# Hybrid decoder layer on one core: attention by half chunks in two turns, TensorE in program order

## The chip, the cores and the metric

The kernel runs on one core of one Trainium2 chip. The metric is the device time of one launch in microseconds (us), taken as the median of several runs; lower is better. The core has a matrix engine (TensorE, in the profile PE for its matmuls and PEld for its weight loads), three engines for elementwise work (VectorE, in the profile DVE; ScalarE, ACT; GpSimd, POOL) and a queue engine (SyncE, SP). [...]

## The reference: what is computed

One inference step of one decoder layer, for a new sequence of 4096 tokens and for 64 sample tokens (8 sequences of 8) with caches. The core of it, cut to what matters here:

```
h = rmsnorm(x, g_pre);  z = h @ w_in                  # 1024 -> combined projection
out_a = silu(g) * B * conv3(C * h_in)                 # 256 channels
out_b = silu(ag) * window_attention(q, k, v, sink)    # 8 heads in 2 kv groups, window 128, 128-query blocks
out_c = silu(mg) * memory_attention(mq, mk, mv)       # 4 heads, 256 memory tokens
y = concat(out_a, out_b, out_c) @ w_out               # width 1024 -> 1024
x = x + rmsnorm(y, g_post)
```

Both attentions are softmax attentions with head size 64. The window softmax has one extra sink logit per head, and a query block of 128 tokens sees its own block and the one before it.

## The kernel before, in words

**Precision.** fp32 values are split into a high and a low float32r part (names ending in hi/lo, mh/ml), and a product is made of three or four matmuls of parts. The scores use full 128-row operands: 64 rows carry the high and 64 rows the low part of a query, against keys stored likewise (`load_queries`, L1115; `load_keys`, L1100).

**Stages.** `input_projection` (L936) does the combined projection in three phases (matmuls at L368) and puts queries, keys, values and gates into DRAM. In its third phase it also makes the memory keys and values and the attention of chunk 0. `open_attention` (L1004) then opens the pools of the last stage. In this stage the output projection of 33 blocks of 128 tokens (`Block.run`, L1476; 32 blocks of the prompt, one of the sample tokens) is interleaved with the attention of chunks 1 to 15 (256 tokens, two half chunks each).

**A block of the output projection.** Its input, the gated mix, is split into mh and ml (`Block.split`, L1461). Two accumulations of 128x512 (p = 0, 1) have 24 matmuls each: for k = 0 to 7 three of them (mh, ml, mh against the high, high, low part of w_out, L1492). The result is multiplied by the norm's gain on VectorE (L1499), squared and summed on ScalarE (L1500); then come a power on GpSimd (L1506), the residual sum on VectorE (L1510) and the store.

**The attention before.** It comes in units. A window unit (`window_unit`, L1237) is one block of 128 queries and one kv group: 8 score matmuls 128x256 into two one-bank tiles `ws` (L1246); a copy and a predicated copy out of PSUM per tile (L1248, L1249); the softmax on VectorE and ScalarE (L1251 to L1264: maximum, exponentials, sum, reciprocal, product); 4 transposes (L1269); a copy (L1271) and two masks on GpSimd (L1276, L1279). A memory unit (`cross_unit`, L1173) is one head of a chunk: 4 score matmuls 128x256 (L1182), maximum, exponentials (L1183 to L1187), the factors on GpSimd (L1191), 4 transposes (L1197) and two copies (L1201). The products with the values are made per half chunk (L1088 for the memory, L1218 and L1224 for the window) into one two-bank tile, followed by the gates on VectorE (L1227, L1170). The class `Pipe` (L1050) hands out one unit at each call of `start` (L1525), and in later calls its factors, transposes and products.

**What sets the order.** `Block.run` calls `start` at k = 2 and k = 6 of each accumulation, in blocks 0 and 1 at k = 0, 2, 4, 6. The order on all engines in this stage is then set by the framework's scheduler, TensorE's too, from priorities in the program's order and its own estimates; on each engine instructions run strictly in the order that results. PSUM has four pools in this stage: `s` (scores) and `t` (transposes) of two one-bank tiles each, `z` (output products) of two one-bank tiles, `pv` (values) of one two-bank tile. GpSimd issues the loads of queries and keys (L1110, L1121), SyncE the others. From block 26 on, the attention of the sample tokens is done in steps at the same calls (`late_start`, L1562).

## Time and profile before

| what | value |
|---|---|
| median of 3 runs | 1538.47 us (1533.01 to 1540.08) |
| the profiled execution's own time | 1536.4 us |
| its span, first to last instruction | 1534.7 us |
| granted TensorE clock | 1.0 of full speed |
| first output product matmul | at 931.2 us of the span |
| last output product matmul | at 1528.2 us of the span |

The profile was taken in one execution. The busy shares are those of the whole span; a busy PE is not PE at its peak, since the ends of matmuls are modelled and matmuls overlap. So where the prediction needs the cost of a matmul it takes the distance from one start to the next, and where it needs a chain on the other engines it takes durations. Rows of the views have the source line of the kernel before, the engine, the operation, output and inputs by tile name, and shapes.

### The profile page before, as it was taken

The numbers are of one execution on the slowest core, as the hardware profiler recorded it, in microseconds if no ns is written. First come the engines' busy times: TensorE is split into PE (matmuls) and PEld (weight loads), VectorE is DVE, ScalarE is ACT, GpSimd is POOL, SyncE is SP. The second block draws the span as 40 slices with busy tenths as digits, with TensorE's granted clock in tenths as the row PEclk, the third lists the DMA queues.
The fourth block names the chain that finished last, engine by engine and source line by source line (L and its number), as shares of the span: only waits on it lengthen the run. The fifth ranks groups of instructions, "written<-read, shape, count | busy, mean of one in ns | idle before, by whom it ended". The sixth has DMA issues, their size and how long they took to land.

```text
span 1534.7 us, 30168 instructions
## 1 busy us (share of the span) xinstructions
PE 1521.5 (99%) x11341; PEld 1399.5 (91%) x11341; DVE 1145.5 (75%) x2055; ACT 805.7 (52%) x2039; POOL 376.1 (25%) x603
## 2 busy tenths in 40 slices
PE   9999999999999999999999999999999999999998
PEld 9999999999999999999999998788888888888877
DVE  6788887899988777897777678766666666666743
ACT  6675665475322222354454447655666556565632
POOL 0223332211300000000101203544444444444310
PEclk9999999999999999999999999999999999999999
DMA  9989999878855333677877789977777777777333
GB/s 265 194 222 225 283 284 266 272 242 298 193 181 180 126 126 126 220 230 280 227 273 230 229 293 254 231 161 153 156 148 148 151 162 149 158 160 150 130 110 96
DMA packets 177942, 306.28 MB, mean 200 GB/s; under 512 B 33925, under 2 KB 107653, under 8 KB 177765
## 3 DMA queue, kind: packets, MB, share of 16 engines
q1 hardware_dynamic: 130901, 227.38, 48.2%
q0 software_dynamic: 46176, 75.92, 25.5%
q8 instruction: 90, 1.47, 0.4%
q10 hardware_dynamic: 720, 1.05, 0.2%
q14 instruction: 55, 0.45, 0.1%
HBM read 197.23 MB, written 108.05 MB: 199 GB/s over the span
## 4 chain that ended last, share of the span: by engine, by line
PE 86%; DMA 7%; DVE 4%; issue 1%; ACT 1%; POOL 1%; SPq 0%; ACTq 0%; DVEq 0%; POOLq 0%
PE c L368 47%; PE y L1492 23%; PE ws L1246 4%; DMA nat<-in_x_p 3%; DMA md<-th 2%; PE wo L1088 2%; PE wt L1269 2%; PE xs L1182 2%; PE xt L1197 2%; PE wo L1218 2%; PE wo L1224 1%; PE mem_acc L789 1%; DMA qd<-z 1%; DVE z L375 1%; DMA xr<-in_x_p 0%
## 5 line engine op out<-in xcount | busy, mean ns | idle before, releaser
L1492 PE MATMUL y<-wo,mh 128*128 128x512 f32 (+1 forms) x1040 | 349.8, 399 | 0.0
L375 DVE TENSOR_TENSOR z<-c,z 128x520 f32<-128x520 f32 (+1 forms) x308 | 194.5, 646 | 79.2 <-PE c L368 78.2
L1492 PEld LDWEIGHTS y<-wo,mh 128*128 128x128 f32 x1040 | 194.3, 188 | 39.2 <-issue 2.4
L1492 PE MATMUL y<-wo,ml 128*128 128x512 f32 (+1 forms) x520 | 201.6, 388 | 0.0
L1259 ACT ACTIVATE sm<-sm,wnm 128x128 f32<-128x128 f32 x256 | 99.5, 390 | 61.0 <-DVE wnm L1253 60.2
L1191 POOL TENSOR_SCALAR xp<-xp,xrd 128x256 f32<-128x256 f32 x128 | 74.4, 588 | 209.6 <-DVE xrd L1187 209.6
L1492 PEld LDWEIGHTS y<-wo,ml 128*128 128x128 f32 x520 | 98.2, 189 | 16.3
L1183 DVE TENSOR_REDUCE xmx<-xs 128x2 f32<-128x512 f32 x64 | 44.1, 689 | 59.2 <-PE xs L1182 59.1
L1271 ACT COPY wpt<-wt 128x512 f32<-128x512 f32 x64 | 37.3, 582 | 88.1 <-PE wt L1269 85.6
L1246 PEld LDWEIGHTS ws<-kst,q 128*128 128x128 f32 x512 | 69.9, 190 | 5.3 <-ACT xp L1186 0.7
L1499 DVE TENSOR_TENSOR yn<-y,gpost 128x512 f32<-128x512 f32 (+1 forms) x66 | 45.1, 683 | 39.6 <-PE y L1492 39.3
L1246 PE MATMUL ws<-kst,q 128*128 128x256 f32 x512 | 73.0, 283 | 0.4 <-ACT xp L1186 0.4
L1500 ACT ACTIVATE y<-y 128x512 f32<-128x512 f32 (+1 forms) x66 | 38.6, 584 | 64.2 <-DVE yn L1499 64.2
L737 POOL CAST wmask<-negs 128x256 uint8<-128x256 f32 x1 | 0.9, 864 | 268.3 <-ACT z L377 268.3
L1279 POOL TENSOR_SCALAR_AFFINE_SELECT wpt<-wpt 128x512 f32<-128x512 f32 x64 | 52.7, 824 | 42.1 <-ACT wpt L1271 39.1
L1186 ACT ACTIVATE xp<-xs,xnm 128x256 f32<-128x256 f32 x128 | 58.8, 464 | 7.1 <-DVE xnm L1184 7.1
L1121 POOL DMA_DIRECT2D q<-qd x64 | 42.8, 674 | 70.6 <-DVE wo L186 60.9
L276 ACT ACTIVATE nat<-nat 104x1024 f32<-104x1024 f32 x40 | 42.3, 1057 | 26.1 <-DMA nat<-in_x_p 26.1
L1510 DVE SCALAR_TENSOR_TENSOR xr<-yn,yst,xr 128x1024 f32<-128x1024 f32 (+2 forms) x34 | 43.4, 1280 | 15.5 <-POOL yst L1506 13.2
L1110 POOL DMA_DIRECT2D kst<-qd x64 | 38.6, 616 | 63.5 <-PE xt L1197 41.4
L1249 DVE COPY_PREDICATED sm<-wmask,ws 128x256 f32<-128x256 uint8 x124 | 52.2, 437 | 2.5 <-ACT sm L1248 2.1
L1276 POOL TENSOR_SCALAR_AFFINE_SELECT wpv<-wpt 128x512 f32<-128x512 f32 x62 | 40.2, 648 | 50.6 <-ACT wpt L1271 50.5
(961 smaller groups left out, 5095.5 us busy)
## 6 DMA issues: line engine op xcount, KB each, us to landing
q<-qd POOLq DMA_DIRECT2D x64, 384.0 KB, 7.9
xr<-in_x_p SPq DMA_DIRECT2D x32, 512.0 KB
nat<-in_x_p SPq DMA_DIRECT2D x39, 416.0 KB
o_yp<-xr SPq DMA_DIRECT2D x31, 512.0 KB
md<-th POOLq DMA_DIRECT2D x48, 260.0 KB, 7.9
qd<-zh SPq DMA_DIRECT2D x48, 260.0 KB
qd<-z SPq DMA_DIRECT2D x48, 260.0 KB
kst<-qd POOLq DMA_DIRECT2D x60, 192.0 KB, 5.6
```

The source lines that it names most:

```text
L368: TE.matmul(bank[:, :HW], l, r, start=first and i == 0, stop=last and i == 3 * KH - 1)
L375: add = lambda dst, other: V.tensor_tensor(dst, c, other, op=ALU.add)
L1183: V.tensor_reduce(mx[:, :nb], s, axis=AX.X, op=ALU.max)
L1186: S.activation(p[:, i, :], s[:, i, :], AF.Exp, bias=nm[:, i : i + 1], scale=SCALE, accum_out=den[:, i : i + 1])
L1191: G.tensor_scalar(p[:, i, :], p[:, i, :], rd[:, i : i + 1], 0.5, op0=ALU.mult, op1=ALU.mult)
L1246: TE.matmul(s3[:, hh, :], self.q[:, 4 + 2 * (2 * half + hh) + kvh, i * P : i * P + P], self.kst[:, 2 * kvh + part, i * P : i * P + 2 * P], ...
L1249: V.copy_predicated(sm[:, 2 * half : 2 * half + 2, :], third["wmask"], third["negs"] if first else s3[:, :, 0:P])
L1259: S.activation(sm[:, hh, :], sm[:, hh, :], AF.Exp, bias=nm[:, hh : hh + 1], scale=SCALE, accum_out=den[:, hh : hh + 1])
L1279: G.affine_select(p3, p3, pattern=[[0, 4], [1, P]], compare_op=ALU.is_ge, fill=0.0, base=0, channel_multiplier=-1)
L1492: TE.matmul(acc, self.hl[l][:, k], wo[k][c0 // 512][:, r, c0 % 512 : c0 % 512 + c1 - c0], start=j == 0, stop=j == passes * KT - 1)
L1499: V.tensor_tensor(yn[:m, c0:c1], acc[:m], gpost[:m, c0:c1], op=ALU.mult)
L1510: V.scalar_tensor_tensor(self.xr[:m, cs], yn[:m, cs], st[:m, 3:4], self.xr[:m, cs], op0=ALU.mult, op1=ALU.add)
```

## The change

The attention of the last stage is no longer handed out in units. A half chunk (128 tokens) h is done in two turns, each put between output product matmuls:

- `first_half(h)`: all 16 window score matmuls of the half chunk, into two two-bank tiles, then the 8 transposes of the memory probabilities of half chunk h-1. Then the softmax of the window scores: one copy and one predicated copy of 512 columns per kv group, where there were two of 256. It also starts the loads for the next chunk.
- `second_half(h)`: the 8 memory score matmuls of two heads into one two-bank tile and their softmax, the value products of half chunk h-1, on every second half chunk 2 transposes of the values, and the 8 transposes of the window probabilities; then masks and gates.

The turns of half chunk b + 4 stand in block b at p = 0, k = 4 and at p = 1, k = 4. For the first ones a table, `EARLY`, sets closer places: counted in k's of the output product (16 to a block), half chunk 2 has its turns at 4 and 12, 3 at 14 and 20, 4 at 22 and 28, 5 at 30 and 36, 6 at 38 and 44.

TensorE's order is as written from block 0 to block 25 (`manual_schedule` on PE); from block 26 on, and on the other engines everywhere, the scheduler orders as before. PSUM in this stage: pool `w` of two two-bank tiles (window scores, window transposes and value products in turn), pool `x` of one two-bank tile (memory scores and memory transposes in turn), pool `z` of two one-bank tiles. The queries of a chunk are loaded by six DMAs in place of four, of the same bytes in sum, in another order of halves. The steps of the sample tokens stand at k = 1 and 3 in place of 2 and 6. The number of matmuls is the same in both programs (10901), and TensorE's order is the same up to the first output product, but for 8 window score matmuls that stood ahead of it before.

```diff
-        ps = {tag: ctx.enter_context(tc.tile_pool(name=f"ps{tag}", bufs=1 if tag == "pv" else 2, space=bass.MemoryType.PSUM))
-              for tag in ("s", "t", "z", "pv")}
+        ps = {tag: ctx.enter_context(tc.tile_pool(name=f"ps{tag}", bufs=n, space=bass.MemoryType.PSUM))
+              for tag, n in (("w", 2), ("x", 1), ("z", 2))}
...
+    def two_banks(tag, name):
+        return ps[tag].tile([P, 2, 512], F32, tag=tag, name=name)
...
+            heads = lambda part, j, ts: qd[part, j : j + 2, :, ts].rearrange("j (v d) n -> d j v n", v=2)
             for part in range(2):
-                for hh in range(2):
-                    half = hh if part == 0 else 1 - hh
-                    G.dma_start(self.q[half * 64 : half * 64 + 64, hh::2, :],
-                                  qd[part, 1:7, hh * 64 : hh * 64 + 64, self.ts].rearrange("j p n -> p j n"))
+                for n, (i, j) in enumerate(((0, 1), (4, 3), (8, 5))):
+                    half = (n == 2) ^ part
+                    G.dma_start(self.q[64 * half : 64 * half + 64, i : i + 4, :].rearrange("p (j v) n -> p j v n", v=2),
+                                heads(part, j, self.ts))
...
+        def window_scores(self, i):
+            b = 2 * self.c + i
+            w = [two_banks("w", f"ws{b}_{kvh}") for kvh in range(2)]
...
+            for kvh, col, bank in sorted(tasks):
+                for part in range(2):
+                    TE.matmul(out(kvh, col, bank), q(kvh, col, bank), k(kvh, part), start=part == 0, stop=part == 1)
+            self.ws = w
+
+        def window_probabilities(self, i):
...
+                S.copy(sm4, s4[:, :, :, P : 2 * P])
+                V.copy_predicated(sm4, third["wmask"].unsqueeze(1).to_broadcast([P, 2, 2, P]), s4[:, :, :, 0:P])
+                self.window_softmax(b, kvh, sm)
...
+        def memory_scores(self, i):
+            c, nb = self.c, CT // P
+            x = two_banks("x", f"xs{c}_{i}").rearrange("p h (b k) -> p h b k", b=nb)
...
+            self.xps = [self.cross_softmax(2 * i + hh, x[:, hh]) for hh in range(2)]
+
+        def memory_transposes(self, i):
+            c, self.pts = self.c, [[], []]
+            tx = two_banks("x", f"xt{c}_{i}")
...
+                (S.copy if hh else V.tensor_copy)(pt, tx[:, hh].rearrange("p (a n) -> p a n", a=2))
+
+        def window_turns(self, i):
+            b = 2 * self.c + i
+            self.steps = [[], []]
+            tw = two_banks("w", f"wt{b}")
+            for kvh in range(2):
+                for hh in range(4):
+                    TE.transpose(tw[:, kvh, hh * P : (hh + 1) * P], self.sms[kvh][:, hh, :], ident)
+            for kvh in range(2):
+                self.window_masks(b, kvh, tw[:, kvh], self.steps[kvh])
...
                 for k in range(KT):
-                    if k in starts:
-                        start()
+                    starts.get((p, k), lambda: None)()
...
+    def first_half(h):
+
+        c, i = divmod(h, 2)
+        if c < NCH:
+            chunks[c].window_scores(i)
+        if 2 < h <= 2 * NCH:
+            chunks[(h - 1) // 2].memory_transposes((h - 1) % 2)
+        if c < NCH:
+            chunks[c].window_probabilities(i)
+            if i == 0:
+                chunks[c].values(chunks[c - 1].vts[2])
+                chunk_load(c + 1)
+            elif c + 1 < NCH:
+                chunks[c + 1].load_mix()
+
+    def second_half(h):
+
+        c, i = divmod(h, 2)
+        if c < NCH:
+            chunks[c].memory_scores(i)
+        banks = None
+        if 2 < h <= 2 * NCH:
+            banks = chunks[(h - 1) // 2].products((h - 1) % 2)
...
+        if c < NCH:
+            chunks[c].window_turns(i)
+        if 2 < h <= 2 * NCH:
+            chunks[(h - 1) // 2].gates((h - 1) % 2, banks)
...
+    EARLY = {4: (first_half, 2), 12: (second_half, 2), 14: (first_half, 3), 20: (second_half, 3), 22: (first_half, 4),
+             28: (second_half, 4), 30: (first_half, 5), 36: (second_half, 5), 38: (first_half, 6)}
+
+    def starts_of(b):
+        steps = {n - 16 * b: (f_, h) for n, (f_, h) in EARLY.items() if n // 16 == b}
+        if b >= 2:
+            steps |= {4: (first_half, b + 4), 12: (second_half, b + 4)} if b > 2 else {12: (second_half, b + 4)}
+        return {(n // 8, n % 8): lambda f_=f_, h=h: f_(h) for n, (f_, h) in steps.items()}
...
+    turn = ExitStack()
+    turn.enter_context(tc.manual_schedule(engines={mybir.EngineType.PE}))
     for i in range(31):
-        run(i, late_start if i >= 26 else start, (0, 2, 4, 6) if i < 2 else (2, 6))
+        if i == 26:
+            turn.close()
+        starts = starts_of(i)
+        run(i, starts | ({(p, k): late for p in range(2) for k in (1, 3)} if i >= 26 else {}))
```

On the other engines the order that the scheduler makes of the changed program is, in the regular blocks, for one half chunk. ScalarE: two copies of window scores, copy of a memory transpose tile, 8 window exponentials, square of y_0, 4 memory exponentials, two copies of window transposes, cast mh of the next block, square of y_1. VectorE: predicated copy, maximum, copy of the other memory transpose tile, predicated copy, maximum, y_0 times gain, the two sums, reciprocals and products of the window softmax, the memory maxima (the reciprocal of the first head's sum stands between them), the two gates, y_1 times gain, ml of the next block, residual sum. GpSimd: factors of the memory probabilities, four masks, the power, and between them ten DMA issues per chunk.

More of the change, by code (lines that the diff above doesn't have):

```diff
@@ new lines, in memory_scores @@
+        def memory_scores(self, i):
+            c, nb = self.c, CT // P
+            x = two_banks("x", f"xs{c}_{i}").rearrange("p h (b k) -> p h b k", b=nb)
+            for hh in range(2):
+                q = self.q[:, 2 * i + hh]
+                for n in range(nb):
+                    for part in range(2):
+                        TE.matmul(x[:, hh, n], q[:, n * P : n * P + P], third["mk"][:, part, 2 * i + hh, :], start=part == 0, stop=part == 1)
+            self.xps = [self.cross_softmax(2 * i + hh, x[:, hh]) for hh in range(2)]
@@ new lines, in window_turns, with products @@
+        def window_turns(self, i):
+            b = 2 * self.c + i
+            self.steps = [[], []]
+            tw = two_banks("w", f"wt{b}")
+            for kvh in range(2):
+                for hh in range(4):
+                    TE.transpose(tw[:, kvh, hh * P : (hh + 1) * P], self.sms[kvh][:, hh, :], ident)
+            for kvh in range(2):
+                self.window_masks(b, kvh, tw[:, kvh], self.steps[kvh])
+        def products(self, i):
+            c = self.c
+            banks = two_banks("w", f"wo{c}_{i}")
+            o = banks[:, 0, CT:]
+            both_values(o, *([(third["mkv"][:, kt, 256 + i * P : 256 + (i + 1) * P], self.pts[hh][kt]) for kt in range(2)]
+                             for hh in range(2)))
+            self.band_values(i, self.steps, banks[:, :, :CT], gated=False)
+            return banks
@@ L1474, in split, with run @@
             self.hl = [hi, lo]
-        def run(self, last, start, split, starts):
+        def run(self, last, starts):
             b, m = self.b, self.m
@@ L1550, in run @@
             blocks[i].split()
-        blocks[i].run(i == len(blocks) - 1, start, split if i == 1 else lambda: None, starts)
+        if i == 1:
+            starts[1, 4] = lambda before=starts[1, 4]: (before(), split())
+        blocks[i].run(i == len(blocks) - 1, starts)
     stages = [sample_mem(0), sample_mem(1), sample_window()]
@@ L1560, in hybrid_layer, with late @@
     quarter = [0]
-    def late_start():
-        start()
+    def late():
         if quarter[0] == 0:
```

162 lines of the change are left out of this document (85 added, 77 removed).

## Prediction

> **What bounds the kernel now.** I read the page first, then the busy time by stretches, then the order in time of each engine where the change is.
>
> ```profile
> PE 1521.5 (99%) x11341; PEld 1399.5 (91%) x11341; DVE 1145.5 (75%) x2055; ACT 805.7 (52%) x2039; POOL 376.1 (25%) x603
> PE 86%; DMA 7%; DVE 4%; issue 1%; ACT 1%; POOL 1%; SPq 0%; ACTq 0%; DVEq 0%; POOLq 0%
> ```
>
> The first line is the busy time of each engine, the second the chain that ended last: TensorE sets the end. The stretches (length, then busy time of PE, PEld, DVE, ACT, POOL, granted clock, DMA) tell where it does not:
>
> ```profile
> 945.00:960.00 15.00, 13.23 (x89) 9.82 (x90) 10.91 (x32) 10.54 (x44) 9.56 (x17) 1.00 1.10 319
> ...
> 1000.00:1400.00 400.00, 400.00 (x2467) 327.17 (x2465) 270.17 (x677) 238.08 (x876) 182.43 (x283) 1.00 0.77 154
> ...
> 1520.00:1535.00 15.00, 8.43 (x60) 7.77 (x58) 4.72 (x9) 1.72 (x7) 1.10 (x2) 0.95 0.29 88
> ```
>
> In the stage that changes (from 930 us) TensorE never rests from 1000 to 1400 us. It waits at the stage's start, and at its end, which the change leaves alone. But a busy TensorE may hide slack, so I read the starts of its matmuls, in a stretch with one of everything (start, duration, count):
>
> ```profile
> 1099.73 1.00 PE L1246 MATMUL ws<-kst,q 128*128 128x256 f32 x7
> 1100.57 0.60 PE L1197 MATMUL xt<-ident,xp 128*128 128x128 f32 x4
> 1100.93 0.47 PE L1492 MATMUL y<-wo,mh 128*128 128x512 f32 x1
> 1101.24 0.40 PE L1492 MATMUL y<-wo,ml 128*128 128x512 f32 x1
> 1101.48 0.62 PE L1492 MATMUL y<-wo,mh 128*128 128x512 f32 x2
> 1101.94 0.39 PE L1492 MATMUL y<-wo,ml 128*128 128x512 f32 x1
> 1102.17 0.62 PE L1492 MATMUL y<-wo,mh 128*128 128x512 f32 x2
> ...
> 1103.78 0.63 PE L1182 MATMUL xs<-mk,q 128*128 128x256 f32 x4
> 1104.34 1.08 PE L1088 MATMUL wo<-xpt,mkv 128*64 128x256 f32 x8
> ...
> 1106.81 0.66 PE L1269 MATMUL wt<-ident,sm 128*128 128x128 f32 x4
> ```
>
> A window score takes 0.12 us (0.84 for 7), an output product 0.23 (0.69 for three from 1101.48), a memory score 0.12, the values of a half chunk 2.47 (1104.34 to 1106.81) and 0.09 before them. Four transposes and the first product after them take 0.67 (1100.57 to 1101.24); less 0.23 that leaves 0.11 each. So a block with its half chunk needs 48 x 0.23 + 16 x 0.12 + 8 x 0.12 + 17 x 0.11 + 2.56 = 18.35 us. It has 113 matmul records; 2467 of them in 400 us are 18.3 us a block. Sum and measurement agree: going from product to attention and back costs nothing, and there is no hidden wait.
>
> [...]
>
> **The change part by part.** The sum is made against the profiled execution's own 1536.4 us (span 1534.7); the median of the runs is 2.1 us above that.
>
> *Fewer groups, other order.* Both builds have 10901 matmuls. By the sum above the regular blocks stay at 18.35 us, as long as nothing makes TensorE wait: 0 us.
>
> *Waits in regular blocks.* TensorE is in program order now, so a late operand stops the products behind it. These rows price the chains (out, in, count, busy us, mean ns):
>
> ```profile
> L1191 POOL TENSOR_SCALAR xp<-xp,xrd 128x256 f32<-128x256 f32 x20 | 12.3, 621 | 33.8 <-DVE xrd L1187 33.8
> L1186 ACT ACTIVATE xp<-xs,xnm 128x256 f32<-128x256 f32 x22 | 10.1, 463 | 0.0
> L1249 DVE COPY_PREDICATED sm<-wmask,ws 128x256 f32<-128x256 uint8 x22 | 9.3, 434 | 0.0
> L1264 DVE TENSOR_TENSOR sm<-sm,wrd 128x512 f32<-128x512 f32 x12 | 8.2, 687 | 0.2
> L1510 DVE SCALAR_TENSOR_TENSOR xr<-yn,yst,xr 128x1024 f32<-128x1024 f32 x6 | 7.7, 1285 | 2.2 <-POOL yst L1506 2.2
> L1183 DVE TENSOR_REDUCE xmx<-xs 128x2 f32<-128x512 f32 x11 | 7.6, 689 | 12.2 <-PE xs L1182 12.2
> L1500 ACT ACTIVATE y<-y 128x512 f32<-128x512 f32 x11 | 6.5, 588 | 11.0 <-DVE yn L1499 11.0
> L1271 ACT COPY wpt<-wt 128x512 f32<-128x512 f32 x11 | 6.4, 583 | 16.7 <-PE wt L1269 16.7
> L1201 DVE COPY xpt<-xt 128x256 f32<-128x256 f32 x11 | 4.6, 420 | 1.9 <-PE xt L1197 1.9
> L1506 POOL TENSOR_TENSOR yst<-yst,mhalf 128x1 f32<-128x1 f32 x5 | 2.8, 564 | 0.0
> L1263 DVE RECIPROCAL wrd<-wden 128x4 f32<-128x4 f32 x12 | 2.1, 178 | 0.4
> ```
> ```profile
> 1208.90 0.40 ACT L1259 ACTIVATE sm<-sm,wnm 128x128 f32<-128x128 f32 x1 [1.32 <-DVE wnm L1253]
> ...
> 1210.37 0.19 ACT L1259 ACTIVATION_READ_ACCUMULATOR sm<-sm,wnm 128x1 f32 x1
> ```
>
> Four window exponentials take 1.66 us, first start to last end. Two forms are new: a 512-column copy on ScalarE (I take 0.58 of L1271) and a 512-column predicated copy. That lies between one and two of 0.434; I take 0.70, since 256 columns more cost 0.27 (0.420 against 0.687).
>
> Time from the start of a first turn: the scores end at 0.96 and 1.92. First kv group: copy to 1.75, predicated copy 2.45, maximum (as L1183) 3.15, copy of the memory transposes that stands next on VectorE 3.85, small operation 4.0, exponentials 6.0; second group's exponentials 7.7; sum, reciprocal, product (0.18 + 0.18 + 0.69) 8.75. TensorE wants it after 1.92 + 0.88 (transposes) + 24 x 0.23 + 0.96 + 2.56 + 0.44 = 12.3: **3.5 us early**. Memory: scores end at 9.5; maximum and small operation 10.4, two exponentials 11.5, reciprocal, second maximum 12.5, exponentials 13.7, reciprocal and factors 15.1; wanted at 18.35 + 1.92 = 20.3. Copies of the window transposes end at 14.9; the tile is wanted at 19.3. The slowest tail is the output's: y_1 ends at 15.7; gain (0.69), square (0.59 + 0.19), sum, power (0.56, perhaps behind a DMA issue of 0.7), residual (1.29) end by 19.9, and the next predicated copy, behind it on VectorE, is wanted at 20.1. Lateness there does not add up from block to block, since each round starts from TensorE's y_1. So 0 us.
>
> *The start.* The dense stretch has 14 kinds of matmul rows from 930.2 to 990 us, of which these are the first and the last, and the causes of the waits:
>
> ```profile
> L1492 PE MATMUL y<-wo,mh 128*128 128x512 f32 x76 | 26.2, 402 | 0.0
> ...
> L368 PE MATMUL c<-hi_7T,w_2A 128*128 128x260 f32 x1 | 0.3, 282 | 0.0
> ```
> ```profile
> 932.44 3.75 DVE L409 TENSOR_TENSOR z<-z,zh 128x520 fp32r<-128x520 f32 x6
> 936.11 1.23 DVE L1473 TENSOR_TENSOR ml<-place,mh 128x1024 fp32r<-128x1024 f32 x1
> ...
> 956.28 1.63 DVE L1510 SCALAR_TENSOR_TENSOR xr<-yn,yst,xr 128x1024 f32<-128x1024 f32 x1 [2.26 <-DMA xr<-in_x_p]
> ```
>
> The view counts 114 products, 77 window and 32 memory scores, 64 transposes and three value groups; at the distances above these and the two L368 are 54.2 of 59.8 us: **5.6 us are lost** now, and only these the change can win. What takes their place: products start where the 8 scores ahead of them stood, at 930.3, and half chunk 2 at 933.0; but VectorE is busy until 937.3 with the rows shown. Its softmax then needs 7.2 us (two predicated copies and two maxima 2.6, exponentials 3.5, sum, reciprocal and product 1.1), to 944.5, and the second group's transposes are wanted at 933.0 + 1.92 + 5.52 + 0.96 + 0.22 + 0.44 = 942.1: 2.4 us. Six products later the second head's factors are behind four masks on GpSimd: 0.9. Half chunk 3 meets the residual row, which cannot start before its load lands at 956.3; behind it 1.29 and 1.7 for the second group end at 959.3, wanted at 958.3: 1.0. Then a score tile waits for a copy behind the fourth head's exponentials: 0.8. Together 5.1; later halves are in time. That is -0.5 us in sum. It lies between -5.6 (no wait) and +8 (each half as late again in the five dense half chunks).
>
> *Smaller edits.* Six query loads for four cost GpSimd two issues more per chunk, hidden under its idle time (182.43 of 400 us busy). At the end the single `x` tile serves the sample steps' nine transposes too; one that waited for a copy would cost up to 0.58, all nine 5, none 0; I take 0.5, since the scheduler spreads them.
>
> Sum: 1536.4 + 0 - 0.5 + 0.5 = 1536.4; the median should stand a little above the profiled execution, as before (2.1 us): I say **1537**.
>
> **The rivals.**
> (a) *The start runs clean.* VectorE catches up and the four waits vanish: 1536.4 - 5.6 = 1531. For it: fewer VectorE instructions. Against it: the chain of 7.3 us.
> (b) *Returns cost after all.* The first product after transposes is 0.31 from the next (1100.93 to 1101.24), 0.08 more than the rest. If that is a loss, halving four returns per block saves 0.16 x 30 = 4.8: 1532, with (a) 1526. Against it: the transposes before it are that much shorter.
> (c) *The window softmax is late in every regular block.* The wait moves into the second turn, before the transposes of the second kv group. It decides from 3.5 us over my chain on; each 0.5 beyond costs 28 x 0.5 = 14: 1551 or slower. For it: fourteen hand-overs that I price at little, and VectorE starting late behind the residual. Against it: predicated copies at twice 0.434 (+0.3), hand-overs of 0.05 (+0.7) and a residual one power and issue late (+1.3) are still 2.3.
> (d) *The start is worse.* Five dense half chunks wait 1.5 to 2 us more each, the loads among them: 1546. The granted clock stayed at 1.00 from 945 to 960 us, where TensorE waits 1.8 us. [...]
> That the change doesn't do what it says can be left out: the built program has TensorE's order as written up to block 25.
>
> **How the numbers follow.** Forecast (1533 to 1541) 0.62, (a) 0.11, (b) 0.04, (c) 0.11, (d) 0.12. Range: from (a) with part of (b), 1529, to (c) at 0.5 us, 1551. Over 0.5% (7.7 us, about what can be told from no change) faster, under 1530.8, takes (b) with (a) and the edge of (a): 0.06. Slower, over 1546.2, takes (c) and half of (d): 0.17. Within: 0.77.
>
> **What would show it.** Right: TensorE busy throughout 1000 to 1400 us with a block every 18.35 us; waits of 1 to 3 us before the transposes of half chunks 2 and 3 only. Wrong: a wait of TensorE for VectorE's window product in each block (c), a distance between products other than 0.23 (b), or a last product well before or after 1528 us.

## The result, and the profile after

| kernel | median (lowest to highest) | ratio to before, 95% interval |
|---|---|---|
| before | 1535.59 us (1533.01 to 1540.08), 22 runs | |
| after | 1539.73 us (1537.76 to 1546.10), 22 runs | 1.003 [1.0021, 1.0039] |

The changed kernel is 4.1 us slower. That lies inside the half per cent that the prediction took as the measure of no change; with 22 runs of each the interval still excludes no change: the kernel became a little slower, where the forecast had it the same or a little faster. The profiled execution of after took 1542.23 us, its span is 1540.5 us. Both profiles hold 11341 matmul records (the count of 10901 given ahead stands in no profile; the two kernels are equal by either).

The page's busy line and chain of waits, and the stretches that the prediction showed of before:

```profile
PE 1520.5 (99%) x11341; PEld 1400.9 (91%) x11341; DVE 1158.9 (75%) x1965; ACT 795.4 (52%) x1949; POOL 395.1 (26%) x635
PE 78%; DMA 10%; DVE 5%; ACT 2%; issue 2%; POOL 1%; SPq 0%; DVEq 0%; ACTq 0%; POOLq 0%
```
```profile
945.00:960.00 15.00, 13.24 (x78) 11.22 (x80) 10.15 (x29) 10.50 (x43) 8.26 (x15) 0.89 1.23 332
1000.00:1400.00 400.00, 400.00 (x2478) 328.56 (x2477) 282.22 (x612) 228.61 (x806) 193.13 (x308) 1.00 0.75 154
1520.00:1535.00 15.00, 13.18 (x81) 11.71 (x79) 5.62 (x11) 3.59 (x11) 1.10 (x2) 1.00 0.24 71
```

TensorE still never rests between 1000 and 1400 us. Between 945 and 960 us it does the same busy time as before (13.24 against 13.23) with 78 matmul records in place of 89, at a granted clock of 0.89. The weight loads' share in the middle is 82% in both kernels.

To place the difference I cut the last stage at four marks: the last matmul of the input projection (L368), the gain of y_1 of block 8, the gain of y_1 of block 24, and the last product. Before, then after, in order of time (the two product rows are the last ones):

```profile
930.15 0.28 PE L368 MATMUL c<-hi_7T,w_2A 128*128 128x260 f32 x1
...
1112.55 0.69 DVE L1499 TENSOR_TENSOR yn<-y,gpost 128x512 f32<-128x512 f32 x1 [0.92 <-PE y L1492]
...
1406.29 0.69 DVE L1499 TENSOR_TENSOR yn<-y,gpost 128x512 f32<-128x512 f32 x1 [0.92 <-PE y L1492]
...
1528.15 0.28 PE L1492 MATMUL y<-wo,mh 128*128 128x256 f32 x1
```
```profile
932.97 0.28 PE L368 MATMUL c<-hi_7T,w_2A 128*128 128x260 f32 x1
...
1117.97 0.69 DVE L1564 TENSOR_TENSOR yn<-y,gpost 128x512 f32<-128x512 f32 x1 [1.59 <-PE y L1557]
...
1410.37 0.69 DVE L1564 TENSOR_TENSOR yn<-y,gpost 128x512 f32<-128x512 f32 x1 [1.59 <-PE y L1557]
...
1532.90 0.28 PE L1557 MATMUL y<-wo,mh 128*128 128x256 f32 x1
```

The differences of these rows, and the same for every kernel of the experiments (us; "start", "blocks 9 to 24" and "last blocks" lie between one mark and the next; "end" is from the last product to the end of the span; "sum" is the sum of the four less that of before, 604.5; "measured" is the median less that of before on the same chip; the ratio is taken over all runs, so the two can differ by 1 us). Between the marks before and after have the same matmuls, but for two transposes of 0.1 us that after has in the start and before in the last blocks:

| kernel | start | blocks 9 to 24 | last blocks | end | sum | measured | ratio, 95% interval |
|---|---|---|---|---|---|---|---|
| before | 182.4 | 293.7 | 121.9 | 6.5 | 0 | 0 | |
| after | 185.0 | 292.4 | 122.5 | 7.6 | +3.0 | +4.1 | 1.0030 [1.0021, 1.0039] |
| a_loads4 | 184.6 | 298.1 | 124.0 | 7.5 | +9.7 | +10.1 | 1.0068 [1.0054, 1.0082] |
| b_loads6 | 184.0 | 293.7 | 121.9 | 7.3 | +2.3 | +2.3 | 1.0017 [1.0007, 1.0028] |
| a_gentle | 182.1 | 292.4 | 122.7 | 7.6 | +0.2 | +1.7 | 1.0013 [1.0003, 1.0023] |
| a_free | 190.0 | 292.4 | 122.7 | 7.8 | +8.4 | +8.4 | 1.0062 [1.0045, 1.0079] |
| a4_order | 186.6 | 292.4 | 122.8 | 7.5 | +4.8 | +4.6 | 1.0031 [1.0019, 1.0044] |
| a_gentle2 | 185.1 | 292.4 | 122.7 | 7.7 | +3.3 | +5.5 | 1.0034 [1.0020, 1.0049] |
| a4_all | 185.4 | 292.4 | 122.5 | 7.6 | +3.3 | +5.1 | 1.0030 [1.0015, 1.0045] |
| a_fill | 185.2 | 292.4 | 122.7 | 7.6 | +3.4 | +3.7 | 1.0029 [1.0015, 1.0043] |
| a_tok | 181.9 | 292.4 | 122.7 | 7.6 | +0.1 | +2.1 | 1.0019 [1.0005, 1.0034] |
| a_tok2 | 187.4 | 292.4 | 122.7 | 7.7 | +5.6 | +8.3 | 1.0054 [1.0035, 1.0073] |
| a_tok4 | 188.0 | 292.4 | 122.7 | 6.5 | +5.1 | +7.4 | 1.0050 [1.0031, 1.0070] |
| a_four | 185.7 | 300.3 | 122.5 | 7.7 | +11.6 | +13.7 | 1.0095 [1.0074, 1.0117] |
| a_tail26 | 185.2 | 292.4 | 126.0 | 7.9 | +6.9 | +8.7 | 1.0048 [1.0033, 1.0064] |
| a_best | 182.5 | 292.4 | 126.0 | 6.5 | +2.9 | +4.7 | 1.0023 [1.0008, 1.0037] |
| a_best2 | 183.0 | 292.4 | 122.8 | 6.5 | +0.2 | +0.3 | 1.0001 [0.9988, 1.0013] |
| a_best3 | 187.5 | 292.4 | 122.7 | 6.5 | +4.6 | +4.3 | 1.0038 [1.0023, 1.0053] |

So after loses 2.6 us in the start, wins 1.3 in sixteen regular blocks, loses 0.7 in the last blocks and 1.1 behind the last product. What lies ahead of the first mark is not compared, since one profile differs from the next there: the mark lies between 926.9 and 939.7 us in these kernels, whose TensorE order up to it is the same.

The start of after, TensorE's rows that follow a wait, and the granted clock (the number behind the five busy times) around the first:

```profile
944.18 0.38 PE L1616 MATMUL vtp<-ident,vT 128*128 128x128 f32 x2
946.29 0.63 PE L1334 MATMUL wt<-ident,sm 128*128 128x128 f32 x4 [1.73 <-ACT sm L1255]
947.39 1.09 PE L1334 MATMUL wt<-ident,sm 128*128 128x128 f32 x4 [0.47 <-DVE sm L1260]
...
949.13 1.05 PE L1557 MATMUL y<-wo,mh 128*128 128x512 f32 x2
949.98 0.58 PE L1557 MATMUL y<-wo,ml 128*128 128x512 f32 x1
```
```profile
964.33 1.87 PE L1292 MATMUL ws<-kst,q 128*128 128x256 f32 x11 [0.73 <-issue]
...
978.53 0.74 PE L1292 MATMUL ws<-kst,q 128*128 128x256 f32 x4 [0.71 <-ACT wpt L1270]
...
994.16 1.09 PE L1292 MATMUL ws<-kst,q 128*128 128x256 f32 x7 [1.60 <-DVE mix L1350]
```
```profile
946.00:948.00 2.00, 1.24 (x7) 1.06 (x8) 1.46 (x6) 1.86 (x9) 0.09 (x1) 0.74 1.17 374
948.00:950.00 2.00, 2.00 (x8) 1.61 (x7) 0.83 (x2) 1.49 (x5) 1.67 (x4) 0.50 1.27 363
950.00:952.00 2.00, 2.00 (x15) 1.86 (x14) 0.17 (x1) 0.71 (x4) 2.00 (x4) 0.90 1.48 256
```

TensorE waits for the window softmax of half chunk 2 (gaps of 2.0 and 0.74 us between starts); then the two products of 949.13 take 0.85 us to the next start, 0.43 each in place of 0.23, at a granted clock of 0.50. Three times later the scores of a new half chunk find no free tile of pool `w` (gaps of 1.1, 1.1 and 1.9 us). Below, "net" is a gap less the distance that the two starts have without a wait.

### The profile page after: what moved, and what is told of

It is laid out like the page before. It is cut to its first block, busy times and chain, and to the rows that moved or that the text cites. A ratio compares the mean times of both kernels' runs of the same rounds, so it can differ in the third digit from the quotient of the medians.

```text
span 1540.5 us, 30049 instructions
## 1 busy us (share of the span) xinstructions
PE 1520.5 (99%) x11341; PEld 1400.9 (91%) x11341; DVE 1158.9 (75%) x1965; ACT 795.4 (52%) x1949; POOL 395.1 (26%) x635
## 4 chain that ended last, share of the span: by engine, by line
PE 78%; DMA 10%; DVE 5%; ACT 2%; issue 2%; POOL 1%; SPq 0%; DVEq 0%; ACTq 0%; POOLq 0%
PE c L368 40%; PE y L1557 23%; PE ws L1292 4%; DMA md<-th 3%; DMA nat<-in_x_p 2%; PE wo L1057 2%; PE xs L1313 2%; PE wt L1334 2%; PE xt L1322 2%; PE wo L1211 2%; PE wo L1217 1%; DVE z L375 1%; DMA hd_B<-place 1%; PE mem_acc L789 1%; DMA x_0B<-in_xt 1%
## 5 line engine op out<-in xcount | busy, mean ns | idle before, releaser
L1557 PE MATMUL y<-wo,mh 128*128 128x512 f32 (+1 forms) x1040 | 336.7, 394 | 0.0
L1161 POOL TENSOR_SCALAR xp<-xp,xrd 128x256 f32<-128x256 f32 x128 | 60.0, 477 | 208.8 <-DVE xrd L1153 208.8
L1092 POOL DMA_DIRECT2D q<-qd x96 | 60.3, 636 | 118.5 <-DVE wo L186 60.4
L1278 POOL TENSOR_SCALAR_AFFINE_SELECT wpt<-wpt 128x512 f32<-128x512 f32 x64 | 66.0, 1050 | 42.0 <-ACT wpt L1270 41.9
L1301 ACT COPY sm<-ws 128x512 f32<-128x512 f32 x60 | 35.2, 587 | 67.7 <-PE ws L1292 67.5
L1292 PEld LDWEIGHTS ws<-kst,q 128*128 128x128 f32 x480 | 61.4, 191 | 6.7 <-DVE mix L1350 1.8
L1292 PE MATMUL ws<-kst,q 128*128 128x256 f32 x480 | 63.0, 283 | 3.1 <-DVE mix L1350 1.6
L377 ACT COPY z<-c 128x520 f32<-128x520 f32 (+1 forms) x44 | 24.3, 553 | 51.7 <-PE c L368 46.4
L407 ACT CAST zh<-z 128x520 fp32r<-128x520 f32 x56 | 33.3, 624 | 33.9 <-DVE z L375 29.5
L1255 ACT ACTIVATION_READ_ACCUMULATOR sm<-sm,wnm 128x1 f32 x256 | 48.5, 190 | 0.0
```

The source lines that it names most:

```text
L1092: G.dma_start(self.q[64 * half : 64 * half + 64, i : i + 4, :].rearrange("p (j v) n -> p j v n", v=2), heads(part, j, self.ts))
L1161: G.tensor_scalar(p[:, i, :], p[:, i, :], self.rds[h][:, i : i + 1], 0.5, op0=ALU.mult, op1=ALU.mult)
L1255: S.activation(sm[:, hh, :], sm[:, hh, :], AF.Exp, bias=nm[:, hh : hh + 1], scale=SCALE, accum_out=den[:, hh : hh + 1])
L1278: G.affine_select(p3, p3, pattern=[[0, 4], [1, P]], compare_op=ALU.is_ge, fill=0.0, base=0, channel_multiplier=-1)
L1292: TE.matmul(out(kvh, col, bank), q(kvh, col, bank), k(kvh, part), start=part == 0, stop=part == 1)
L1557: TE.matmul(acc, self.hl[l][:, k], wo[k][c0 // 512][:, r, c0 % 512 : c0 % 512 + c1 - c0], start=j == 0, stop=j == passes * KT - 1)
```

## The experiments

**First four: loads, density, program order.** The profile of after had a wait of 2.3 us at 777 us, ahead of the changed stage, with half a clock for 3.4 us behind it, and the query loads are the only part of the change that reaches there. So the loads were the first theory, the dense start the second. a_loads4 puts the four loads back, b_loads6 puts the six into the kernel before:

```diff
-                for n, (i, j) in enumerate(((0, 1), (4, 3), (8, 5))):
-                    half = (n == 2) ^ part
-                    G.dma_start(self.q[64 * half : 64 * half + 64, i : i + 4, :]...
+                for hh in range(2):
+                    half = hh if part == 0 else 1 - hh
+                    G.dma_start(self.q[half * 64 : half * 64 + 64, hh::2, :], ...
```

> The changed kernel with the four query loads of before in place of six, in all chunks; nothing else. Theory 1 (the loads): in the changed kernel TensorE waits 2.3 us at 776.7 us, in the stage before the change, for VectorE, which waited 2.65 us for the store qd<-zh to land behind the loads of chunk 0; after it the products come 0.216 us apart in place of 0.119 for 3.4 us. Together 3.8 us: this kernel should have no such wait and take 1539.7 - 3.8 = 1536 us, 1.000 of before. Theory 2 (only the dense start costs, the wait at 777 us is chance): 1539 to 1540 us, and the wait is there again or is gone from other kernels with six loads too.

> The kernel before with the six query loads, nothing else of the change. Theory 1 (the loads): a wait of about 2.2 us near 777 us and some 3 us of half clock behind it, 1535.6 + 3.8 = 1539.4 us, ratio 1.0025. Theory 2 (only the dense start costs): 1535.6 us, ratio 1.000, no wait near 777 us.

Measured: a_loads4 1545.87 us, **6 us slower** than after, with no wait at 777 us; b_loads6 1538.06 us, 2.3 us slower than before, and no wait at 777 us either. Theory 1 falls. The gap near 777 us is there in after (2.3 us), a_gentle (0.7), a_tok (0.6) and a_tok2 (1.3), all with six loads, and in a_best3 (1.4) with four, and under 0.4 us in the others: it comes and goes. What six loads cost in the kernel before is in the table: 1.6 us in the start and 0.7 behind the last product. But the scheduler also gave that kernel another order, on TensorE and VectorE too: it has gaps of 1.8 and 1.7 us at 972 and 991 us, where before has one of 2.0 at 960. So the 1.6 us is not the price of the added issues alone. In the trace's events GpSimd's closing drain ends 6.5 us behind the last product in each kernel with six loads and 5.8 in each with four (in a_loads4, a4_order and a4_all SyncE's wait for the last store was 1.1 us longer, so that their end is 7.5 nevertheless).

In a_loads4 the loss lies in the regular blocks (298.1 against 292.4). From the first mark on, TensorE, ScalarE and GpSimd (its DMA issues aside) have the same order as in after; only VectorE's differs. VectorE and TensorE there, first after, then a_loads4, one half chunk each:

```profile
1176.66 1.29 DVE L1575 SCALAR_TENSOR_TENSOR xr<-yn,yst,xr 128x1024 f32<-128x1024 f32 x1 [1.60 <-POOL yst L1571]
1177.86 0.73 DVE L1302 COPY_PREDICATED sm<-wmask,ws 128x512 f32<-128x512 uint8 x1
1178.62 0.69 DVE L1247 TENSOR_REDUCE wmx<-sm 128x4 f32<-128x512 f32 x1
...
1180.43 0.41 ACT L1255 ACTIVATE sm<-sm,wnm 128x128 f32<-128x128 f32 x1
...
1184.25 0.69 DVE L1260 TENSOR_TENSOR sm<-sm,wrd 128x512 f32<-128x512 f32 x1
...
1187.22 1.04 PE L1334 MATMUL wt<-ident,sm 128*128 128x128 f32 x8
```
```profile
1324.93 1.29 DVE L1573 SCALAR_TENSOR_TENSOR xr<-yn,yst,xr 128x1024 f32<-128x1024 f32 x1 [2.24 <-POOL yst L1569]
1326.13 1.35 DVE L1300 COPY_PREDICATED sm<-wmask,ws 128x512 f32<-128x512 uint8 x2
1327.35 0.69 DVE L1324 COPY xpt<-xt 128x512 f32<-128x512 f32 x1
1327.94 1.29 DVE L1245 TENSOR_REDUCE wmx<-sm 128x4 f32<-128x512 f32 x2
...
1329.34 0.40 ACT L1253 ACTIVATE sm<-sm,wnm 128x128 f32<-128x128 f32 x1 [0.67 <-DVE wnm L1247]
...
1333.16 0.69 DVE L1258 TENSOR_TENSOR sm<-sm,wrd 128x512 f32<-128x512 f32 x1
...
1333.99 0.63 PE L1332 MATMUL wt<-ident,sm 128*128 128x128 f32 x4 [0.44 <-DVE sm L1258]
```

In after the second product ends at 1184.94; the transposes that read it begin about 1187.7 (four of 0.11 us behind 1187.22): 2.7 us early. In a_loads4 both predicated copies stand ahead of both maxima, the first exponential comes 3.1 us after the residual's end in place of 2.5, and TensorE waits. VectorE's order has this form in every second half chunk. The lead of the product over its transposes (from its end to their start), read at each half chunk, falls in steps: 3.2, 2.0, 1.4, 0.8, 0.1 us every two blocks, and stays there.

a_gentle has the same work with half chunks further apart. In it blocks 2, 4 and 6 are split ahead of their second memory gate, so two memory heads go ungated into these blocks' products: it leaves out the wait for these gates, and serves for the start alone. a_free drops TensorE's program order:

```diff
# a_gentle
+    EARLY = {4: (first_half, 2), 13: (second_half, 2), 15: (first_half, 3), 22: (second_half, 3), 24: (first_half, 4), 31: (second_half, 4), 36: (first_half, 5), 44: (second_half, 5), 50: (first_half, 6), 57: (second_half, 6), ...
# a_free
-    turn.enter_context(tc.manual_schedule(engines={mybir.EngineType.PE}))
```

> The changed kernel with another table for the first half chunks: turns of 2 to 10 at 4/13, 15/22, 24/31, 36/44, 50/57, 62/70, 75/83, 88/96, 102/110 in k's, so that the regular place is reached at half chunk 11 in place of 7; six loads as in the changed kernel. Theory 2 (the dense start costs): the waits before the scores at 963, 977 and 992 us (1.0, 1.0 and 1.8 us) go, the one at 944 us shrinks by 0.7 and with it 1 us of half clock: 4 to 6 us less, 1534 to 1536 us. The wait at 777 us stays. If the dense start is not what costs, under 1 us less, 1539 to 1540 us.

> The changed kernel without the program order on TensorE: the scheduler orders it in all blocks, from the same half-chunk groups, places and pools; six loads. If the program order makes the start wait, the scheduler puts other products into the waits at 944 to 993 us and the kernel gains up to 6 us, 1534 us. If the waits come from the groups' size and the two-bank tiles, it stays at 1539 to 1540 us. If the order as written is what makes a regular block 18.27 us in place of 18.35, the regular blocks lose 1.5 to 2 us again.

Measured: a_gentle 1537.41 us, its start 2.9 us shorter than after's, without the wait for these gates; a_tok below has the same table with it. a_free 1544.14 us: its start is 5 us longer, with one wait of 5.3 us before the first value products, whose cause the trace does not name. Its regular blocks take 292.4 us like after's. So program order is not what makes a regular block shorter, and in the start it is better than the scheduler's.

**Next four: VectorE's order, a slower table with all gates, the parts together, the clock.** a4_order adds one edge to a_loads4:

```diff
+                if kvh:
+                    tc.add_manual_dep(late.ins, self.top.ins.name, mybir.DependencyInfo(...NoSync...), reason="order")
```

> The changed kernel with four query loads, and one order on VectorE: the predicated copy of the second kv group stands behind the maximum of the first. Theory A (VectorE's order): with four loads the scheduler had put both predicated copies ahead of both maxima in every second half chunk; the first exponential came 3.1 us after the residual's end in place of 2.5, the lead of the window product over its transposes shrank by 0.6 us every two blocks, from 3.2 us to nothing, and then TensorE waited 0.65 us every two blocks. With the order of the changed kernel the lead should stay near 2.7 to 3.1 us, two blocks should take 36.5 us in place of 37.15, and the time falls from 1545.9 to about 1539. Theory B (the four bigger loads hold GpSimd, its power and the residual behind it): the lead shrinks again, 1545 to 1546 us.

Measured: 1540.46 us, 5.4 us less than a_loads4, 292.4 us in the regular blocks, the lead at 2.7 to 3.0 us (once 2.4). Theory A is **shown**, and theory B falls, since the four loads are in place: one order of two instructions on VectorE is worth 5.7 us over 16 blocks.

```diff
# a_gentle2
+    EARLY = {4: (first_half, 2), 13: (second_half, 2), 15: (first_half, 3), 21: (second_half, 3), 22: (first_half, 4), 28: (second_half, 4), 33: (first_half, 5), 41: (second_half, 5), 44: (first_half, 6), ...
+        if i == 3:
+            starts[1, 0] = split
```

> The changed kernel, six loads, with a slower table that keeps every gate ahead of its split: half chunks 2 to 7 have their turns at 4/13, 15/21, 22/28, 33/41, 44/52, 57/65, and block 4 is split at the middle of block 3. If the dense start costs: the waits before scores at 977 and 992 us go (3 us), the one at 944 us shrinks by 0.7, the one at 963 us stays: 1.5 to 3 us less than the changed kernel's 1539.7, 1537 to 1538. If it does not: 1539 to 1540 us.

Measured: 1541.27 us, no gain. The waits at 977 and 992 us are gone and another has come, inside the products, at the first ones of block 2:

```profile
973.76 0.49 PE L1557 MATMUL y<-wo,mh 128*128 128x512 f32 x1 [0.63 <-ACT mh L1540]
975.08 0.50 PE L1557 MATMUL y<-wo,ml 128*128 128x512 f32 x1 [0.82 <-DVE ml L1541]
```

Block 2 waits for its own mh and ml. They stand behind the gates of `second_half(4)`, since a memory turn makes two heads for all 256 tokens, so a block of chunk 1 needs the turns of both its half chunks and one more. In after the turn of half chunk 5 stood ahead of block 2 and covered it. So a slower table alone does not help: the time goes into the chain from half chunk 2 to block 2.

```diff
# a4_all: a4_order, a_gentle2's table, and in sample_mem
-        t = psum("t", f"smot{bh}")
+        t = psum("pv", f"smot{bh}")
```

> All together: four loads, the order on VectorE, the slower table, and the sample tokens' last transposes in a tile of pool w in place of the single x tile. By the parts: 1539.7, less 0.7 (GpSimd's last drain is 0.74 us shorter in kernels with four loads), less 2 (slower table), less 1.1 (the wait at 1474 us for the x tile) is 1536 us, 1.000 of before. If the parts overlap or move waits elsewhere, 1537 to 1539 us.

Measured: 1540.93 us. Its start has gentle2's waits, and at 1476 us the wait for the x tile became one for the next step's transposes (gap 1.1 us).

```diff
# a_fill, in second_half behind the value transposes
+            if h == 2:
+                for n in range(16):
+                    TE.transpose(banks[:, 0, n % 4 * P : n % 4 * P + P], ident, ident)
```

> The changed kernel with 16 more transposes that nobody reads, right behind the value transposes of half chunk 2, where TensorE waits 2.0 us. If the half clock from 948 to 950.4 us comes from the idle time, TensorE is busy 1.76 us longer, the 0.74 us wait alone is left, the products behind it are 0.23 us apart at once, and the start is 1.1 us shorter (too little for the times, to be seen in the starts of the matmuls). If it comes from something else, the products are 0.43 us apart again and the time is the same or up to 1.8 us longer.

Measured: 1539.55 us. The gap of 2.0 us is filled, the granted clock stays at 1.00 from 941 to 951 us, but half chunk 3's transposes then wait (a gap of 1.25 us) and the start is no shorter. It does not settle why the clock falls: a_four has the same two gaps (2.0 and 0.74 us) unfilled and keeps 1.00 too. But both show what the half clock cost here: nothing. Half chunk 4's scores start 31.4 us behind the first mark in after, 31.5 in a_four and 31.6 in a_fill. At the full clock TensorE waits for VectorE instead:

```profile
959.87 0.63 PE L1334 MATMUL wt<-ident,sm 128*128 128x128 f32 x4 [0.87 <-DVE sm L1260]
```

This row is a_four's, the second transposes of half chunk 3; after has no wait there.

**Next four: the chain cut, and the returns.** a_tok has a_gentle's table and cuts half chunk 4 out of block 2's chain:

```diff
-                for n in range(nb):
+                    h, t = (2 * hh + n, i) if c <= 5 else (2 * i + hh, n)
...
+            if self.c <= 5:
+                gate = self.mix[:, 2:4, i * P : i * P + P]
# a_tok2, a_tok4
+    EARLY = {4: (first_half, 2), 15: (second_half, 2), 17: (first_half, 3), 25: (second_half, 3), 27: (first_half, 4), 36: (second_half, 4), ...
# a_four, from block 8 on
+            steps = {4: (part(first_half, 0), b + 4), 6: (part(first_half, 1), b + 4),
+                     12: (part(second_half, 0), b + 4), 14: (part(second_half, 1), b + 4)}
```

> The changed kernel with the table of a_gentle, in which half chunks come further apart, made valid: in chunks 1 to 5 a memory turn does four heads for its own 128 tokens in place of two heads for 256, so that block 2 needs half chunks 2 and 3 alone, and no longer 4 (the values of the memory are then 16 matmul records of half the columns in place of 8). Theory C (block 2 waits for a chain through half chunk 4): a_gentle's start is kept, the stage from the last L368 to the last product takes 597 to 598 us against 599.9 of the changed kernel, and the time is 1537 to 1538 us. If a_gentle's start came only from its too early split, the stage takes 600 us again: 1539 to 1540 us.

Measured: the stage takes 597.0 us as expected (start 181.9), the time is 1538.4 us, ratio 1.0019 against 1.0030 of after. Theory C is shown in the stage: a_gentle's start is kept with all gates, and block 2's waits are gone. The start is 3.1 us shorter than a_gentle2's, of which these waits are 1.9. The medians of 12 runs barely tell it, and the dense table with the chain cut was not run.

> As a_tok, with the second turn of half chunk 2 two k's later and 3 to 5 at 17/25, 27/36, 38/46, and block 3 split in the middle of block 2. By theory C the 1.6 and 0.7 us waits at 942 us shrink to under 1 us, the half clock behind them stays away, and nothing else is late: the stage takes 596 us, the time is 1536 us. If VectorE is late again at the next place, 1537 to 1538 us.

> As a_tok2, with four query loads and the order of VectorE from a4_order. If the six loads cost only at GpSimd's last drain (0.74 us), 1535 us, at or under the 1535.8 of before; if four loads make the start 1.6 us longer as in a4_order, 1537 us.

Measured: 1544.61 and 1543.66 us, starts of 187.4 and 188.0. Two k's more for half chunk 2 than in a_tok save 0.6 us there and cost waits of 2.8 and 2.5 us before the next scores. Each turn's copies on ScalarE are wanted by the next turn, and everything behind half chunk 2 moves with it.

> The changed kernel with each turn cut in two from block 8 on: window scores at k = 4, memory transposes at 6, memory scores and products at 12, window transposes at 14, so four returns to the products in a block as before the change, where the changed kernel has two. If a return costs about 0.08 us (two fewer in a block are 0.083 us, 18.275 against 18.358 us by the starts of the products' readers over 16 blocks), the regular blocks take 18.36 us again and the kernel 1.5 us more, 1541 us. If the gain of the regular blocks is from something else (program order, wider copies), they stay at 18.275 us and the kernel at 1539.7.

Measured: 1550.05 us, 300.3 us in the regular blocks. Most of this is a wait that the cut made: the memory transposes' copy on ScalarE is late for the memory scores every second half chunk (gap 0.95 us, 0.36 us a block net).

```profile
1371.85 0.39 PE L1313 MATMUL xs<-mk,q 128*128 128x256 f32 x1 [0.55 <-ACT xpt L1326]
```

What is left speaks for returns: the distance from product to product (those under 0.25 us) is on average 229.9 ns before, 227.8 in after and 229.0 in a_four. 46 of them at 2.1 ns are 0.10 us a block, where after won 0.083. But a_four, with as many returns as before, lies between the two, and the wait is mixed in. So this is argued more than shown.

**Last four: the end, and the sum of the named parts.**

```diff
# a_tail26, a_best
-        run(i, starts | ({(p, k): late for p in range(2) for k in (1, 3)} if i >= 26 else {}))
+        run(i, starts | ({(p, k): late for p in range(2) for k in (2, 6)} if i >= 26 else {}))
# a_best3
+    EARLY = {4: (first_half, 2), 15: (second_half, 2), 16: (first_half, 3), 22: (second_half, 3), ...
```

> The changed kernel with the sample tokens' steps at k = 2 and 6 as before the change. From the end of block 24's second gain to the last product the changed kernel needs 122.54 us and the kernel before 121.87. If the places of the steps cost, 121.9 again and no wait of 1.1 us before the memory transposes at 1474 us; if the single x tile costs, whose readers the transposes wait for, 122.5 to 122.7 and the wait stays. Either way the time is within 1 us of 1539.7.

Measured: 126.0 us in the last blocks: the places of before are worse here (a gap of 2.7 us before the samples' memory scores). So the old places do not win the 0.7 us back; it belongs to the single x tile's wait or stays open.

> a_tok (slower table, memory turns by own tokens in chunks 1 to 5) with four query loads, VectorE's order, and the sample steps at k = 2 and 6. If the parts add up: stage 597.0, less up to 0.7 for the tail, GpSimd's drain 0.74 us shorter: 1535 us, 0.3 to 1 us under before, which the times can hardly tell from 1.000. If four loads change the start again (y_1 of block 8 came 1.6 us later with them in a4_order): 1536 to 1538 us.

> a_best with the sample steps back at k = 1 and 3: at 2 and 6 the last blocks took 126.0 us in place of 122.5, with a wait of 2.7 us before the samples' memory scores. By the parts of a_best's own trace the stage takes 600.9 - 3.3 = 597.6 us and the end 6.5, together 604.1 us against 604.5 of the kernel before: ratio 0.999 to 1.001. If something else than the start, the regular blocks, the last blocks and the end is slower in the changed kernel, 1.002 or more.

> a_best2 with the second turn of half chunk 2 at 15 and the first of 3 at 16, all else the same. If the wait before the transposes of half chunk 2 (1.8 us) is all that changes, it shrinks by up to 1.4 us: stage 596.3, ratio 0.998 to 1.000. If half chunk 3 is late in its place, the stage takes 597.5 to 599 us, 1.000 to 1.002.

Measured: a_best 1539.01 us, with a_tail26's 126.0 in it; a_best2 1536.75 us, **ratio 1.0001 [0.9988, 1.0013]**: with the named parts changed, these runs tell no difference, to about 2 us either way. A finer sum is not shown: by its profile a_tok is as level (+0.1 against +0.2), yet its ratio is 1.0019. a_best3 1540.78 us: the waits before half chunk 2's transposes shrink by 0.8 us (2.3 to 1.5 net), and one of 3.2 us appears behind them, before the memory scores of half chunk 3. No version came out under before.

## Why the prediction was right or wrong

- **Regular blocks: right in what limits them, 0.083 us off in size.** No wait from 1000 to 1400 us; 18.275 us a block in after against 18.358 (292.40 and 293.73 over 16). The prediction put the gain of two fewer returns (from attention back to products) at nothing, rival (b) at 0.16 us. Half of (b) came true in size; that it is the returns is argued, as a_four left it.
- **The window softmax: 2.7 to 3.1 us early (once 2.5) where 3.5 was forecast.** But "lateness there does not add up from block to block, since each round starts from TensorE's y_1" is wrong as a rule. In a_loads4 it adds up: the residual stands behind GpSimd's power, that behind masks and factors, those behind the softmax of the round before. This loop was 0.6 us longer than two blocks of TensorE, and within eight blocks the lead was gone. Rival (c) was one order of VectorE away, and its point of decision was not the lead but the loop's length.
- **The start: the step that failed is "later halves are in time".** Forecast -0.5 us, measured +2.6. The first term was right to 0.1 us: 2.4 us for half chunk 2 (2.00 and 0.74 less two regular distances of 0.11 are 2.5), though both groups of transposes waited and not the second alone. The terms of 0.9 and 1.0 do not show in after, where the half clock held five products back by 1.1 us in their place; at the full clock, in a_four, they are 0.3 and 1.0 net. The fourth, 0.8, came out at 1.1: the first eight scores at 963 us waited 0.9 for the memory gate on VectorE, and the others for the copy behind the exponentials, which ended last (at 965.52, the ninth score starts at 965.58):

```profile
963.82 0.41 DVE L1350 TENSOR_TENSOR mix<-mix,wo 128x256 f32<-128x256 f32 x1
```
```profile
964.94 0.58 ACT L1270 COPY wpt<-wt 128x512 f32<-128x512 f32 x1
```

  "Later halves are in time" was put at nothing and fails at 977 us (0.9 net) and at 992 us (1.8 net): 2.7 us. So the waits did not stay with the transposes of half chunks 2 and 3, as the prediction's sign of being right had it; three stand before scores. With these 2.7 us the forecast for the start would have been +2.2; the other 0.4 is not placed. At 977 us it is the fourth term's mechanism again, the copies of the window transposes behind the exponentials of a memory head:

```profile
976.96 0.47 ACT L1152 ACTIVATE xp<-xs,xnm 128x256 f32<-128x256 f32 x1
```
```profile
977.41 1.07 ACT L1270 COPY wpt<-wt 128x512 f32<-128x512 f32 x2
```

  The wait at 992 us is for the memory gate. The gate that frees the tile stands behind a residual of 2.48 us, itself behind a power that stands behind two query issues:

```profile
988.92 1.24 POOL L1092 DMA_DIRECT2D q<-qd  x2 [4.43 <-issue]
990.15 0.60 POOL L1571 TENSOR_TENSOR yst<-yst,mhalf 128x1 f32<-128x1 f32 x1
...
992.32 2.03 POOL L1275 TENSOR_SCALAR_AFFINE_SELECT wpv<-wpt 128x512 f32<-128x512 f32 x2
```
```profile
990.79 2.48 DVE L1575 SCALAR_TENSOR_TENSOR xr<-yn,yst,xr 128x1024 f32<-128x1024 f32 x1 [0.24 <-POOL yst L1571]
993.20 0.59 DVE L1150 TENSOR_SCALAR xnm<-xmx 128x2 f32<-128x2 f32 x1
993.70 0.41 DVE L1350 TENSOR_TENSOR mix<-mix,wo 128x256 f32<-128x256 f32 x1
```

  In a_loads4 one issue stands there, the residual takes 1.33 us and the gap is 0.9 us in place of 1.9. In a4_order, with four loads too, it is 2.1: there another VectorE operation took 1.48 us beside GpSimd's masks.

  Rival (d) was the nearest: a worse start, the loads among the causes. It gave 1.5 to 2 us more to each of five half chunks; only the one at 992 us was that much later than forecast.
- **Query loads: "hidden under its idle time" failed.** In the kernel before alone they cost 2.3 us [1.1 to 4.3 by the interval]: 0.7 in GpSimd's closing drain, and 1.6 in the start together with the order that came with them. In the changed kernel, taking them back with VectorE's order held won nothing (a4_order 1.0031, after 1.0030).
- **The tail: right in size, its cause shown in part.** +0.5 forecast, +0.7 measured in the last blocks. The wait for the x tile's readers is there (gap 1.1 us at 1474 us), one of more than the 0.58 that the prediction gave to one. Without it the last blocks took no less: 122.5 us in a4_all, where the wait moved. The 1.1 us behind the last product were in no term: 0.7 of them is the drain.
- **The clock.** The forecast had no term for a lower clock. In the kernel before the granted clock stayed at 1.00 behind the gap of 2.0 us; in after it fell to 0.50 for 3.4 us behind gaps of 2.0 and 0.74 us. In this start the fall did not change the time: half chunk 4's scores start 31.4 us behind the first mark in after, and 31.5 in a_four at 1.00.

## What to carry to other kernels

A start-up table shifts waits about as long as the chain to the first consumer stays as long: find what the first late block needs, and cut that dependence along with moving turns. A lead that looks ample in one round is no proof of a steady state: follow the loop through the other engines back to itself and compare its length with the bound engine's period. And put every edit that looks like plumbing (two more DMAs) into the kernel before, alone: it may cost, or reorder another engine. Before a slow stretch is charged with lost time, look whether the next wait would have taken it anyway.

## What the runs showed of the hardware

- **The clock.** After a wait the granted clock fell to 0.50 for 3.4 us in after (gap of 2.3 us at 777 us; 2.0 and 0.74 at 944), a4_all (1.8 at the same place), and a_tail26 and a_best (2.7). From 930 to 1000 us it was 0.98 on average in after and in a_loads4, and 0.95 in a4_order. It fell from within the wait on, and for longer, in a_best3 (gap of 3.6; at 0.50 from 956.9 to past 963 us) and a_free (5.6; from 959.9 to past 965 us). It stayed at 1.00 behind gaps of 2.0 (before), 2.0 and 0.74 (a_four), 1.8 (a_best2), and 2.8 and 2.5 us (a_tok2). So in these runs the length of one gap between 1.8 and 2.8 us does not decide; the fall came with both of these gaps over 3 us. What else decides was not shown.
- **PSUM.** In before and after VectorE and ScalarE read the tiles that TensorE wrote, and no row of GpSimd does. Its window masks work on ScalarE's copy (`wpt<-wt`, 0.58 to 0.61 us for 128x512 in after) and wait for it (26.2 us in sum in before, from 1000 to 1400 us); its factors work on the exponentials (`xp<-xp,xrd`, 0.47 us for 128x256 in after).
- **VectorE beside GpSimd.** The residual takes 1.28 to 1.29 us in 30 of its 31 full-width runs in after, and 2.48 in the one that ran beside two factors and a mask of GpSimd. 26 of after's masks take 1.6 us in place of 0.6, all of them beside the subtraction for ml. The trace has them side by side; what slows them was not shown.
